# Macaron block on one core: the FFN's engine order listed from block 0's up product, nine more Strassen quads in each FFN, 31 of its first sums made by adding DMAs

## Chip, cores and metric

One NeuronCore of a Trainium2 chip. The metric is the device time of one execution in microseconds, taken as the median of three runs. Everything is fp32; a product is made from fp32r halves.

## What is computed

```python
f = _swiglu(_rmsnorm(h, ln_ffn1_pre), ffn1_gate, ffn1_up, ffn1_down)   # (silu(x@Wg) * (x@Wu)) @ Wd
h = h + 0.5 * _rmsnorm(f, ln_ffn1_post)
mx = _hybrid_mixer(_rmsnorm(h, ln_mix_pre), w_in, ...)                 # RWKV-7 scan and pooling
h = h + _rmsnorm(mx, ln_mix_post)
f = _swiglu(_rmsnorm(h, ln_ffn2_pre), ffn2_gate, ffn2_up, ffn2_down)
h = h + 0.5 * _rmsnorm(f, ln_ffn2_post)
```

There are 256 tokens of width 2048, and the FFN is 5632 wide. So each FFN reads three weights of 2048 x 5632 once.

## The kernel before

**A product in three matmuls.** Each fp32 operand is split into a high fp32r part H and a rest L. `mm3` (L317 to L321) makes one product of a 128-row slice as H·H, H·L and L·H, three matmuls with 512 columns. ScalarE casts H out of the loaded weight, and VectorE subtracts to get L (`fetch`, L373 and L383, two 128-row slices k at a time: 128 x 1024 elements). The tiles wH and wL come from a ring of five.

**Seven products for eight.** `seven` (L508) works on two blocks of 512 output columns at once, named f and l: gate and up in the first part of an FFN, two column blocks of the down weight in its second part. A letter f or l in its order string is a *pair*: two k of one weight for both halves of the tokens, 12 matmuls. A letter q is a *quad*: two k of both weights, by Strassen's scheme in 7 products (21 matmuls) where two pairs take 24. A quad costs VectorE more: it makes sums of weights, t13 (128 x 1024, L576), t2 and t4 (128 x 512 each, L581 and L585), and takes L from four tiles, a (1024), b (512), t13 and t24 (1024 each) (L598). The matching sums of the tokens (`sums`, L421) are made once for two quads and kept. After the last quad of a block the products' banks are merged on VectorE (L645, L693).

**Stages of an FFN.** Block 0 is the first 512 columns of gate, then of up; blocks 1 to 10 are gate and up together (`GATE_UP`, one order string for each); then the down product in two groups of 1024 output columns (`DOWN`). While block 0 is computed the normed tokens are scaled (`normed`), after each block the result is turned by VectorE, moved across partitions by 16 DMAs from GpSimd (L892) and split (`carry`). `post` makes the closing RMS norm, whose last column block is worked in two halves of tokens (`by_half`). The mixer between the FFNs uses `seven` once, with 4 quads (`OUT`).

**What sets the order.** `Plan` takes a list of operations with engine, cost, dependencies, buffers and due times, plays it through (`solve`) and emits each engine's instructions in that order. Before, the list begins with block 1; block 0, the statistics and the setup of the mixer are emitted outside it. All loads go out on SP's queue in the planned order. The constants at the top (`FETCH`, `UNITS`, `LAT`) are the planner's; 25 units of 4 KB a partition hold sums, kept tiles and loads.

Of the kernel before, what the change touches and what calls it, by code (L numbers as in the profile page):

```python
# [17 lines left out]
P = 128  # L18
# [26 lines left out]
DOWN = ((0, "fffffffffffqfff" "qllqllqllqllqllqllqll", 0),  # L45
        (2, "fqflqfqflqfqflqfqflqfqfqff", TRAIL))
OUT = ((0, "", 0), (1, "fffqfq" "qlqlll", 0), (3, "", TRAIL))
GATE_UP = ["", "ffffffffllllllll"] + ["ffqfqfqlqlll", "fffqffqlqllll", "ffqfqfqlqlll", "fffqffqlqllll", "ffqfqfqlqlll", "fffqffqlqllll", "ffqfqfqlqlll", "fffqffqlqllll", "ffqfqfqlqlll"]
SUMS = (2, 2)
BY_DMA = range(0)  # L50
LAT = dict(PE=0.22, DVE=0.1, ACT=0.17, SP=0.0, POOL=8.0)
AGAIN = dict(PE=0.0, DVE=0.0, ACT=0.0, SP=0.0, POOL=0.0)
UNITS = dict(ffn=25, out=22)
FIFO = dict(pt=4, pm=4, tmp=TB)
SPARE, KEEP, URGENT, HOLD = 3, 4, 8.0, 99
SOON, FETCH, LATEST, BEFORE = 22.0, 22.0, 12.0, 12.0
EARLY = 0.5
NXSPARE = 1
# [31 lines left out]
class Plan:  # L90


    def __init__(s):
        s.fifos = {r: [] for r in FIFO}
        s.nodes, s.last, s.chain, s.clk = [], None, {}, 0.0
        s.units, s.inserts = UNITS["out"], []
        s.begin = s.pe(BEFORE, lambda: None)
# [39 lines left out]
    def solve(s):  # L137
# [16 lines left out]
        free = dict(w32=[0.0] * W32_BUFS, ring=[BEFORE - 12 * MM * i for i in range(WS_BUFS)][::-1], unit=[0.0] * s.units)  # L154
# [29 lines left out]
        while len(order) < len(s.nodes):  # L184
            best = None
            for e, c in front.items():
                got = [(when(n), n) for n in c]
                if got:
                    first = min(a for a, _ in got)
                    a, n = min((x for x in got if x[0] <= first + 1e-9),  # L190
                               key=lambda x: x[1].due)
                    if best is None or a < best[0]:
                        best = (a, n)
# [27 lines left out]
class Block:  # L221
    def __init__(s, tc, ctx):
# [5 lines left out]
        s.late, s.after = [], []  # L228
# [38 lines left out]
    def run(s):  # L267

        E = mybir.EngineType
        with s.tc.manual_schedule(engines={E.PE, E.Activation, E.DVE, E.SP, E.Pool}):  # L270
            for n in s.plan.solve():
                n.fn()
            s.stats()
        s.plan, s.ready = Plan(), {}
# [42 lines left out]
    def mm3(s, ps, aH, aL, bH, bL, start, stop):  # L317
        nc = s.nc
        nc.tensor.matmul(ps, aH, bH, start=start, stop=False)  # L319
        nc.tensor.matmul(ps, aH, bL, start=False, stop=False)  # L320
        nc.tensor.matmul(ps, aL, bH, start=False, stop=stop)  # L321
# [80 lines left out]
    def by_half(s, w, c0, k0, k1, do, keep, done=None, deps=(), used=None, ready=None):  # L402
# [3 lines left out]
        for h in range(2):  # L406
            for k in range(k0, k1, 2):
                low, dst = got[k]
                at = []
                if ready is not None:  # L410
# [3 lines left out]
                         [low, *deps, *at],  # L414
# [6 lines left out]
    def sums(s, T, Td, j, out, own=None, nq=2, used=(), x32=None):  # L421
# [13 lines left out]
        def second():  # L435
            x = tt["x"] if x32 is None else x32[0][0].rearrange(
                "p (a b) t -> p a b t", b=2)[:, :nq]
            a11, a21 = x[:, :, 0, :P], x[:, :, 0, P:]
            a12, a22 = x[:, :, 1, :P], x[:, :, 1, P:]
            f = tt["f"] = s.unit((P, 4, nq, P), F32, "sf")  # L440
            V.scalar_tensor_tensor(out=f[:, 0], in0=a21, scalar=-1.0, in1=a22, op0=ALU.mult,
                                   op1=ALU.subtract)
            V.scalar_tensor_tensor(out=f[:, 1], in0=f[:, 0], scalar=-1.0, in1=a11,
                                   op0=ALU.mult, op1=ALU.subtract)
            V.tensor_tensor(out=f[:, 2], in0=a11, in1=a21, op=ALU.subtract)
            V.tensor_tensor(out=f[:, 3], in0=a12, in1=f[:, 1], op=ALU.subtract)
# [53 lines left out]
        else:  # L500
            b = p.op("DVE", 4 * cost("DVE", size / 4), second, [Td[j], p.chain.get("sums")],
                     [kf], [x32[1]], ahead=SOON, spare=NXSPARE)
        c = p.op("ACT", cost("ACT", size, 0.1 * (n - 1)), steps[0], [b, *used], kept)
# [4 lines left out]
    def seven(s, wf, cf, wl, cl, at, dep, KT, need, sm, order, ev_f, ev_l, used, trail=0):  # L508
# [4 lines left out]
        n = order.count("q")  # L513
# [4 lines left out]
        left = dict(f0=std + n, f1=std, l0=std + n, l1=std + n, p1=n, p5=n, p6=n, p7=n)  # L518
# [9 lines left out]
        def mul(b, x, wt):  # L528
# [5 lines left out]
            s.mm3(bank[b], *x, *wt, new, left[b] == 0)  # L534
# [9 lines left out]
        def pair(k, w, c0, b, by_dma):  # L544
            low, dst = s.fetch(w, k, c0, keep, by_dma, by_dma)

            def do():
                for i in range(2):
                    for h in range(2):
                        mul(f"{b}{h}", rows(k + i, h), ws[k + i])  # L550
            d = p.pe(12 * MM, do, [low, dep(k)] + claim(b + "0", b + "1"), dst)
# [3 lines left out]
        def quad(q):  # L555
# [10 lines left out]
            def get(m):  # L566
                i, x_ = m // 2, "ab"[m % 2]
                if m < 2:
                    v[x_] = raw((ka, kb)[m])
                w, c0 = ((wl, cl), (wf, cf))[(m + i) % 2]  # L570
                nc.sync.dma_start(out=v[x_][:, i],
                                  in_=w[(k + i) * P:(k + i + 1) * P, c0:c0 + 512])

            def t13():
                v["t13"] = s.unit((P, 2, 512), F32, "t13")
                V.tensor_tensor(out=v["t13"], in0=v["a"],  # L576
                                in1=v["b"][:, :1].to_broadcast([P, 2, 512]), op=ALU.subtract)
# [6 lines left out]
            def t4():  # L584
                V.tensor_tensor(out=v["t24"][:, 1], in0=v["b"][:, 1], in1=v["t24"][:, 0],  # L585
                                op=ALU.subtract)
# [9 lines left out]
            def low(n_, m):  # L596
# [3 lines left out]
            ld = [p.op("SP", 0.4, lambda m=m: get(m), take=([ka], [kb], (), ())[m], size=0.26,  # L600
                       chain="SP", ahead=FETCH) for m in range(4)]

            def half(n_, m, deps, rel):
# [5 lines left out]
            n13 = p.op("DVE", two, t13, ld[:3], [k13, k24], [ka, kb])  # L609
            la, ra = half("a", 2, [ld[0], ld[2]], [ka])  # L610
            n2 = p.op("DVE", one, t2, [n13], (), [ka, k13])
# [7 lines left out]
                                  mul("f0", S_(4), x["a"][1])),  # L619
                 [la, ds, dep(k)] + claim("p1", "f0", "f1"), ra)  # L620
            p.pe(3 * MM, lambda: mul("l0", rows(k + 1, 0), x["b"][0]),
                 [lb] + claim("l0", "l1"), rb)
# [3 lines left out]
            d = p.pe(6 * MM, lambda: (mul("p6", S_(2), x["t24"][0]),  # L626
                                      mul("l1", rows(k + 1, 1), x["t24"][1])),
                     [l24] + claim("p6"), r24)
# [13 lines left out]
        def add(o, b, i):  # L642
            if u[o] is None:
                new(o)
            V.tensor_tensor(out=u[o], in0=bank[b], in1=u[i], op=ALU.add)  # L645
        m, use = {}, {}

        def merge(d):
            for i in range(4):
                use[i] = p.claim("tmp")  # L650
            m["u0"] = p.op("ACT", cost("ACT", 512), copy, [d] + use[0][0])
            held["p1"].append(m["u0"])
            d = m["u0"]
            for o, b, i in ((1, "p6", 0), (2, "p7", 1), (1, "p5", 1), (3, "p5", 2)):
                d = m[f"u{o}"] = p.op("DVE", one, lambda o=o, b=b, i=i: add(o, b, i),
                                      [d] + (use[o][0] if o > 1 or b == "p6" else []))
                held[b].append(d)
                use[i][1].append(d)
        nq, last = 0, {}
        ks = dict(f=iter(range(K0, KT, 2)), l=iter(range(K0, KT - trail, 2)))  # L660
        for c in order:
            if c == "q":
                last["q"] = quad(nq)
                nq += 1
                if nq == n:
                    merge(last["q"])
# [7 lines left out]
            if c == "f" and left["f"] == std // 2:  # L674
                m["f"] = last["f"]

                def close_f():
                    for h, i in ((0, 1), (1, 3)):
                        if n:
                            d = p.op("DVE", one, lambda h=h, i=i: add(i, f"f{h}", i),  # L680
                                     [last["f"], m[f"u{i}"], last["q"]])
# [5 lines left out]
                if not n or "u3" in m:  # L687
# [4 lines left out]
        def total(h):  # L692
            V.tensor_tensor(out=u[2 * h], in0=bank[f"l{h}"], in1=u[2 * h], op=ALU.add)  # L693
        if trail:
            def finish(h, d):
                d = p.op("DVE", one, lambda: total(h), [d, m["u0"], m["u3"]], due=p.clk)
                ev_l(h, d, lambda: u[2 * h], None)
            s.by_half(wl, cl, KT - trail, KT, lambda k, h: mul(f"l{h}", rows(k, h), ws[k]),
                      keep, finish, [dep(k) for k in range(KT - trail, KT, 4)],
                      used)  # L700
            return
        for h in range(2):
            if n:
                d = p.op("DVE", one, lambda h=h: total(h), [p.last, m["u0"], m["u3"]])
                held[f"l{h}"].append(d)
                ev_l(h, d, lambda h=h: u[2 * h], use[2 * h][1])
# [3 lines left out]
    def head(s, w, c0, KT, do, keep, xs):  # L710
# [11 lines left out]
        with s.tc.manual_schedule(engines={E.PE, E.Activation, E.DVE, E.SP}):  # L722
# [27 lines left out]
            s.stats()  # L750

    def stats(s):
        while s.late:
            s.late.pop(0)()
# [70 lines left out]
    def rstd(s, ss, n, r):  # L825
        nc = s.nc
        t = s.small(1, "rt", bufs=2)
        nc.vector.tensor_reduce(out=t, in_=ss, axis=AX.X, op=ALU.add)
        t2 = s.small(1, "rt2", bufs=2)
        nc.vector.tensor_scalar(out=t2, in0=t, scalar1=1.0 / n, scalar2=NORM_EPS,  # L830
                                op0=ALU.mult, op1=ALU.add)
        nc.gpsimd.tensor_tensor(out=r, in0=t2, in1=s.mhalf[:, :1], op=ALU.pow)
# [48 lines left out]
    def carry_steps(s, T1, T, x32=None):  # L881

        nc = s.nc
        x, own = [x32], []
# [16 lines left out]
        def high(h):  # L901
            if h == 0:
                own.extend(s.new_T(1))
                T.extend(own)
# [27 lines left out]
    def carry(s, T1, T, turned, k1, by_dma=False):  # L932

        p = s.plan
        move, high, low, whole, minus, add = s.carry_steps(T1, T)
        kx, kT = Tok("unit"), [Tok("unit"), Tok("unit")]
        n = None
# [3 lines left out]
        hs = []  # L941
        for h in range(2):
            hs.append(p.op("ACT", cost("ACT", 512), lambda h=h: high(h), [n] + hs,
                           kT if h == 0 else (), chain="high",
                           spare=KEEP))
        if by_dma:
            for h in range(2):
                n = p.op("ACT", cost("ACT", 512), lambda h=h: whole(h), [n, *hs])
            n = p.op("ACT", cost("ACT", 1024), minus, [n, *hs])
            return p.op("POOL", 1.25, add, [n], (), [kx], size=0.94, lat=ADD), kT  # L950
# [38 lines left out]
    def ffn(s, wg, wu, wd, uT, rs, gpost, resid, emit, reload, xs=None):  # L989
        nc = s.nc  # L990
        hT, sm = [], [None] * 12
# [21 lines left out]
        s.gemm_tok(wg, 0, at, NKD, lambda h, ps: ev_g(0, h, ps), lead=True, xs=xs)  # L1013
# [1001 lines left out]
```

## Time and profile before

| what | value |
|---|---|
| three runs | 2016.54, 2017.03, 2017.33 us; median 2017.03 |
| span of the profiled execution | 2015.4 us, 1.6 us less than the median |
| TensorE instructions | 9957, busy 2000.9 us |
| VectorE / ScalarE / GpSimd busy | 1824.7 / 1192.3 / 327.6 us |
| FFN 1, mixer, FFN 2 (rough borders) | 31 to 707, 707 to 1326, 1326 to 2004 us |

Engines in the profile: PE is TensorE's matmul, PEld its weight load, DVE VectorE, ACT ScalarE, POOL GpSimd, SP the queue of loads. A row of the groups gives line, engine, operation, tiles (out<-in), shape, count, then busy time, mean ns of one, and the idle time before them. A row of the windows gives, for a stretch, the busy time of each engine, the granted clock, the DMA engines' busy share and GB/s. In the timeline the first figure is the start, the second the duration in us, and "xN" merges N instructions. Matmuls are pipelined, so the distance of two starts tells the pace, not the duration of one.

### The profile page before, as it was taken

How to read it: one execution, taken by the hardware profiler on the slowest of the kernel's cores; microseconds unless marked ns; L12 is line 12 of the kernel's file. 1: busy time of each engine (PE TensorE's matmuls, PEld its weight loads, DVE VectorE, ACT ScalarE, POOL GpSimd, SP SyncE). 2: the span in 40 equal slices, each digit the busy share in tenths (PEclk: the TensorE clock that was granted, in tenths of full speed). 3: DMA queues.
4: the chain of work that ended last, by engine and by line, in shares of the span. 5: the costliest groups of instructions: out<-in, count | busy, mean ns of one | idle time of the engine just before them, and what ended most of it. 6: DMA issues, size and time to landing. Idle time of an engine off the chain costs nothing.

```text
span 2015.4 us, 28684 instructions
## 1 busy us (share of the span) xinstructions
PE 2000.9 (99%) x9957; PEld 1655.1 (82%) x9957; DVE 1824.7 (91%) x2424; ACT 1192.3 (59%) x1586; POOL 327.6 (16%) x673
## 2 busy tenths in 40 slices
PE   9999999999999999999999999999999999999997
PEld 7888888888888888888788788888888888888886
DVE  6999999999999957789689678979999999999997
ACT  7555665556666566685476434665656555566663
POOL 0111211131000123403220111011113111310000
PEclk9999999999999999999999999999999999999999
DMA  7675674667568577757456547666656747665683
GB/s 268 224 241 182 220 242 160 218 213 241 175 203 299 209 212 214 205 175 214 146 173 190 159 168 269 244 216 215 228 198 218 245 142 235 211 228 183 207 294 126
DMA packets 227419, 423.56 MB, mean 210 GB/s; under 512 B 24639, under 2 KB 28105, under 8 KB 227273
## 3 DMA queue, kind: packets, MB, share of 16 engines
q1 hardware_dynamic: 204713, 384.70, 57.9%
q0 software_dynamic: 22272, 36.51, 5.5%
q8 instruction: 78, 1.28, 0.3%
q10 hardware_dynamic: 288, 0.52, 0.1%
q14 instruction: 68, 0.56, 0.1%
HBM read 396.69 MB, written 8.39 MB: 201 GB/s over the span
## 4 chain that ended last, share of the span: by engine, by line
PE 97%; DVE 1%; issue 1%; DMA 0%; ACT 0%; POOLq 0%; POOL 0%; DVEq 0%; ACTq 0%
PE mm L319 27%; PE mm L321 26%; PE mm L320 26%; PE ms L320 5%; PE ms L321 5%; PE ms L319 5%; PE tr L849 1%; PE pA L1733 0%; DVE u L645 0%; PE mc L817 0%; DMA x<-in_x_dram 0%; PE pU L1829 0%; PE pSa L1841 0%; PE pY L1864 0%; PE pT L1900 0%
## 5 line engine op out<-in xcount | busy, mean ns | idle before, releaser
L319 PE MATMUL mm<-wH,xH 128*128 128x512 f32 (+1 forms) x2116 | 825.5, 391 | 0.0
L320 PE MATMUL mm<-wL,xH 128*128 128x512 f32 (+1 forms) x2116 | 821.2, 388 | 0.0
L321 PE MATMUL mm<-wH,xL 128*128 128x512 f32 (+1 forms) x2116 | 821.1, 388 | 0.0
L319 PEld LDWEIGHTS mm<-wH,xH 128*128 128x128 f32 x2116 | 397.4, 188 | 82.1
L321 PEld LDWEIGHTS mm<-wH,xL 128*128 128x128 f32 x2116 | 397.4, 188 | 82.0 <-DVE xL L867 0.2
L373 ACT CAST wH<-w 128x1024 fp32r<-128x1024 f32 x313 | 326.2, 1054 | 231.7 <-PE mm L321 208.1
L320 PEld LDWEIGHTS mm<-wL,xH 128*128 128x128 f32 x2116 | 397.7, 188 | 79.7
L383 DVE TENSOR_TENSOR wL<-w,wH 128x1024 fp32r<-128x1024 f32 x313 | 373.0, 1218 | 18.9 <-ACT wH L373 17.3
L593 ACT CAST wH<-t 128x1024 fp32r<-128x1024 f32 x208 | 219.4, 1055 | 217.0 <-PE mm L321 108.9
L296 DVE TENSOR_TENSOR wL<-w,wH 128x1024 fp32r<-128x1024 f32 (+2 forms) x200 | 236.6, 1192 | 95.7 <-ACT wH L295 94.1
L295 ACT CAST wH<-w 128x1024 fp32r<-128x1024 f32 (+2 forms) x200 | 205.4, 1034 | 170.9 <-PE mm L321 150.7
L892 POOL DMA_DIRECT2D x<-T x352 | 173.1, 499 | 729.8 <-DVE T L875 190.3
L598 DVE TENSOR_TENSOR wL<-t,wH 128x1024 fp32r<-128x1024 f32 x208 | 248.6, 1217 | 0.7 <-ACT wH L593 0.7
L593 ACT CAST wH<-w 128x1024 fp32r<-128x1024 f32 x208 | 168.3, 835 | 56.6 <-PE mm L321 30.0
L598 DVE TENSOR_TENSOR wL<-w,wH 128x1024 fp32r<-128x1024 f32 x208 | 194.5, 951 | 0.3
L576 DVE TENSOR_TENSOR t<-w,w 128x1024 f32<-128x1024 f32 x104 | 126.7, 1218 | 0.0
L320 PE MATMUL ms<-wL,sH 128*128 128x512 f32 x276 | 107.6, 390 | 0.2
L319 PE MATMUL ms<-wH,sH 128*128 128x512 f32 x276 | 107.4, 389 | 0.0
L321 PE MATMUL ms<-wH,sL 128*128 128x512 f32 x276 | 107.4, 389 | 0.0
L585 DVE TENSOR_TENSOR t<-w,t 128x512 f32<-128x512 f32 x104 | 71.8, 690 | 2.6
L581 DVE TENSOR_TENSOR t<-w,t 128x512 f32<-128x512 f32 x104 | 71.3, 686 | 0.6
L645 DVE TENSOR_TENSOR u<-ms,u 128x512 f32<-128x512 f32 x92 | 61.4, 686 | 1.4
(317 smaller groups left out, 2107.8 us busy)
## 6 DMA issues: line engine op xcount, KB each, us to landing
w<-in_w_in_dram SPq DMA_DIRECT2D x128, 512.0 KB
w<-in_ffn_up_dram SPq DMA_DIRECT2D x112, 512.0 KB
w<-in_ffn_gate_dram SPq DMA_DIRECT2D x110, 512.0 KB
w<-in_ffn_down_dram SPq DMA_DIRECT2D x104, 512.0 KB
w<-in_ffn_down_dram SPq DMA_DIRECT2D x144, 256.0 KB
w<-in_ffn_gate_dram SPq DMA_DIRECT2D x132, 256.0 KB
w<-in_ffn_up_dram SPq DMA_DIRECT2D x128, 256.0 KB
w<-in_w_out_dram SPq DMA_DIRECT2D x24, 512.0 KB
```

Source lines behind the costliest of these rows:

```text
L295: s.nc.scalar.copy(vH, v)
L296: s.nc.vector.tensor_tensor(out=vL, in0=v, in1=vH.bitcast(F32), op=ALU.subtract)
L319: nc.tensor.matmul(ps, aH, bH, start=start, stop=False)
L320: nc.tensor.matmul(ps, aH, bL, start=False, stop=False)
L321: nc.tensor.matmul(ps, aL, bH, start=False, stop=stop)
L373: nc.scalar.copy(x["H"], x["v"])
L383: nc.vector.tensor_tensor(out=x["L"], in0=x["v"], in1=x["H"].bitcast(F32), op=ALU.subtract)
L576: V.tensor_tensor(out=v["t13"], in0=v["a"], in1=v["b"][:, :1].to_broadcast([P, 2, 512]), op=ALU.subtract)
L585: V.tensor_tensor(out=v["t24"][:, 1], in0=v["b"][:, 1], in1=v["t24"][:, 0], op=ALU.subtract)
L593: nc.scalar.copy(H, src)
L598: V.tensor_tensor(out=L, in0=src, in1=H.bitcast(F32), op=ALU.subtract)
L892: nc.gpsimd.dma_start(out=x[0][q * 32:q * 32 + 32, i], in_=src[i * 32:i * 32 + 32, q])
```

## The change

1. **More quads.** The order strings change, from 50 quads in each FFN to 59 (41 in blocks 1 to 10, two of them in block 1, and 18 in the down product). Block 1 works on the normed tokens as the others do.
2. **Adding DMAs.** A capital Q is a quad whose t13 VectorE does not add: SP loads the two slices into t13, and a DMA from GpSimd then adds the third slice, 512 KB broadcast over both halves, to it in SBUF. The slices a and b are loaded besides, so such a quad loads 5 slices of 256 KB on SP's queue and not 4. There are 31 in each FFN, 24 of them in blocks 1 to 10. Signs are turned so that the sum is an addition.
3. **The list starts earlier.** Block 0's up product, the sums of squares and their powers, the spread of the norm, `normed` and the mixer's setup (whose 12 small loads go from SP's queue to GpSimd's) are operations of the plan.
4. **Merges.** In the last down group the quads' banks are added into the PSUM bank before the last pairs run on, so no sum is left after the last matmul; in one block of each FFN bank l1 is seeded with a sum. The FFN's last squares are summed on ScalarE and no longer on VectorE. The token sums of five of the down product's groups start from a kept fp32 copy, and one addition falls away.
5. **Planner.** VectorE work that uses the result just before it is charged 0.12 us (`AGAIN`), an operation that is due sooner may be awaited 0.13 us (`PATIENCE`).

```diff
-GATE_UP = ["", "ffffffffllllllll"] + ["ffqfqfqlqlll", "fffqffqlqllll", ...]
+GATE_UP = ["", "fffflQlfqfllll", "fqqflQQQfll", "flflQfqqQfll", "flqQfffqQlll", ...]
+            def begin():
+                v["t13"] = s.unit((P, 2, 512), F32, "t13")
+                for i, (w, c0) in enumerate(((wf, cf), (wl, cl))):
+                    nc.sync.dma_start(out=v["t13"][:, i],
+                                      in_=w[(k + i) * P:(k + i + 1) * P, c0:c0 + 512])
+            def adding():
+                nc.gpsimd.dma_start(out=v["t13"], in_=wl[k * P:(k + 1) * P, cl:cl + 512]
+                                    .unsqueeze(1).to_broadcast([P, 2, 512]), accum_op=ALU.add)
...
+            if far:
+                n13 = p.op("SP", 0.8, begin, take=[k13], size=0.52, ahead=FETCH)
+                n13 = p.op("POOL", 1.0, adding, [n13], size=0.94, lat=FAR)
-            n2 = p.op("DVE", one, t2, [n13], (), [ka, k13])
+            n2 = p.op("DVE", one, t2, [n13, ld[0]], [k24] * far, [ka, k13])
...
-        part, direct = [None, None], KT == NKD
+        part, direct = [None, None], True
```

**VectorE in a gate and up block of FFN 1.** Before, in a stretch of two quads: every t13 is made by L576 from two loaded tiles w.

```order
L576 TENSOR_TENSOR t_689_3062<-w_659_2892,w_666_2925 128x1024
L581 TENSOR_TENSOR t_692_3067<-w_659_2892,t_689_3062 128x512
L598 TENSOR_TENSOR wL_3065<-t_685_3026,wH_3064 128x1024
L585 TENSOR_TENSOR t_692_3067<-w_666_2925,t_692_3067 128x512
L576 TENSOR_TENSOR t_696_3081<-w_676_2980,w_677_2982 128x1024
L383 TENSOR_TENSOR wL_3079<-w_652_2868,wH_3078 128x1024
L383 TENSOR_TENSOR wL_3088<-w_655_2873,wH_3087 128x1024
L598 TENSOR_TENSOR wL_3100<-w_659_2892,wH_3099 128x1024
```

In the changed program, at the quads t_571 and t_639 of FFN 1 (L622, L627, L631, L644 are the lines that were L576, L581, L585, L598):

```order
L644 TENSOR_TENSOR wL_2749<-w_596_2560,wH_2748 128x512
L627 TENSOR_TENSOR t_637_2753<-w_599_2567,t_571_2437 128x512
L622 TENSOR_TENSOR t_639_2757<-w_609_2611,w_611_2618 128x1024
L631 TENSOR_TENSOR t_637_2753<-w_604_2588,t_637_2753 128x512
L627 TENSOR_TENSOR t_642_2775<-w_609_2611,t_639_2757 128x512
L644 TENSOR_TENSOR wL_2772<-t_557_2396,wH_2771 128x1024
L631 TENSOR_TENSOR t_642_2775<-w_611_2618,t_642_2775 128x512
```

The quad of t_571 has no L622: its L627 takes a t13 that a DMA has summed. Quads stand closer, and the plain pairs' L383 between them are fewer.

**GpSimd in the same part.** Before, only the moves of `carry` stand there, 16 for a block:

```order
L892 DMA x_384_1654<-T_379_1629 32x256 x16
L892 DMA x_477_2069<-T_471_2036 32x256 x16
L892 DMA x_553_2423<-T_550_2405 32x256 x16
L892 DMA x_658_2887<-T_647_2836 32x256 x16
L892 DMA x_722_3180<-T_717_3160 32x256 x16
```

Now (L982 is the move, L617 the adding DMA):

```order
L982 DMA x_519_2206<-T_506_2153 32x256 x16
L617 DMA t_557_2396<-in_ffn_up_dram 128x2x512
L617 DMA t_571_2437<-in_ffn_up_dram 128x2x512
L982 DMA x_603_2583<-T_583_2498 32x256 x16
L617 DMA t_600_2569<-in_ffn_up_dram 128x2x512
L617 DMA t_626_2705<-in_ffn_up_dram 128x2x512
L617 DMA t_643_2777<-in_ffn_up_dram 128x2x512
```

Adding DMAs and moves share GpSimd's queue, each behind the one before.

**VectorE at the program's end.** Before, for the last half of the tokens: the total (L693), the squares (L1173), the gain (L1159), the outputs (L1182).

```order
L693 TENSOR_TENSOR u_18796<-mm_18047,u_18796 128x512
L1173 ISA junk_18939,rt_2610_13152<-u_18796,rp_18871 128x512
L1173 ISA rt_2610_13152 128x1
L1159 TENSOR_TENSOR fg_13146<-u_18796,gb_13142 128x512
L1182 SCALAR_TENSOR_TENSOR fg_13145<-fg_13145,rs_13151,h_163_694 128x512 x2
L1182 SCALAR_TENSOR_TENSOR fg_13146<-fg_13146,rs_13151,h_164_695 128x512 x2
```

Now, from the first half's outputs on (L1291 the gain, L1302 the norm, L1314 the outputs; ScalarE's squares of mm_18553 stand between L1291 and L1302):

```order
L1314 SCALAR_TENSOR_TENSOR fg_13103<-fg_13103,rs_13109,h_113_447 128x512 x2
L1314 SCALAR_TENSOR_TENSOR fg_13104<-fg_13104,rs_13109,h_114_448 128x512 x2
L1291 TENSOR_TENSOR fg_13106<-mm_18553,gb_13102 128x512
L1302 TENSOR_SCALAR rt_2618_13112<-ss_13108,rp_19186 128x1
L1314 SCALAR_TENSOR_TENSOR fg_13105<-fg_13105,rs_13111,h_115_449 128x512 x2
L1314 SCALAR_TENSOR_TENSOR fg_13106<-fg_13106,rs_13111,h_116_450 128x512 x2
```

The total after the last matmul has gone, and the gain reads the PSUM bank ahead of the squares.

More of the change, by code (lines that the diff above doesn't have):

```diff
@@ L652, in merge, with step @@
             held["p1"].append(m["u0"])
[L653 to L656, printed above, removed]
+            def step(o, b, i, after):
+                d = m[f"u{o}"] = p.op("DVE", one, lambda: add(o, b, i), after + (
+                    use[o][0] if o > 1 or b == "p6" else []))
@@ L941, in carry @@
         hs = []
+        keep.append((x, kx, n))
         for h in range(2):
             hs.append(p.op("ACT", cost("ACT", 512), lambda h=h: high(h), [n] + hs,
[L944 to L950, printed above, removed]
+                           kT if h == 0 else (), chain=None if late else "high",
+                           spare=KEEP, ahead=SOON if late else 1e9))
         for h in range(2):
@@ L1110, in normed @@
         done, toks, own = [], [], {}
-        rows = p.op("ACT", 2.0, lambda: None, [p.begin])
         for i in range(len(uT)):
```

483 lines of the change are left out of this document (306 added, 177 removed).

## Prediction

> **What bounds the kernel now.** I read the page's shares first, then the windows by stage, then the waits of PE. In the page, PE and DVE are the two engines to think of:
>
> ```profile
> span 2015.4 us, 28684 instructions
> PE 2000.9 (99%) x9957; PEld 1655.1 (82%) x9957; DVE 1824.7 (91%) x2424; ACT 1192.3 (59%) x1586; POOL 327.6 (16%) x673
> ```
>
> A PE that is 99% busy need not run at its peak, so its pace comes from the timeline. The first and the last of 77 matmuls in a row, in FFN 1:
>
> ```profile
> 599.72 0.39 PE L320 MATMUL ms<-wL,xH 128*128 128x512 f32 x1
> ...
> 616.95 0.39 PE L321 MATMUL ms<-wH,sL 128*128 128x512 f32 x1
> ```
>
> 76 steps in 17.23 us are 0.2267 us each, for quads and pairs alike. The waits of PE, in full, show that nothing holds this pace up for long:
>
> ```profile
> PE warm L725 <- POOL ident masks.py:199: 1.7, 1, 1.7
> PE tr L849 <- DMA x<-in_x_dram: 1.2, 1, 1.2
> PE pU L1829 <- DVE R L1854: 0.3, 1, 0.3
> ```
>
> The first two are the start of the program, the third is in the mixer. So in the FFNs the time is the number of matmuls times 0.2267 us. How far DVE is from becoming the bound, the windows show: the two FFNs, then their steady parts in the gate and up blocks, and the first 50 us of FFN 2. The columns are the length, then the busy time of PE, PEld, DVE, ACT and POOL, the clock, the DMA engines' share and GB/s.
>
> ```profile
> 31.00:707.00 676.00, 675.89 (x2999) 559.56 (x2998) 658.55 (x778) 405.25 (x487) 97.33 (x194) 1.00 0.65 219
> 1326.00:2004.00 678.00, 677.89 (x2994) 561.14 (x2993) 649.99 (x762) 401.58 (x479) 93.94 (x185) 1.00 0.63 212
> ...
> 100.00:500.00 400.00, 400.00 (x1766) 331.21 (x1765) 395.26 (x455) 237.46 (x269) 78.58 (x160) 1.00 0.65 216
> 1330.00:1380.00 50.00, 50.00 (x223) 41.37 (x222) 36.05 (x40) 29.55 (x43) 11.21 (x18) 1.00 0.79 268
> 1430.00:1830.00 400.00, 400.00 (x1766) 331.35 (x1765) 395.67 (x461) 238.21 (x272) 70.67 (x144) 1.00 0.63 207
> ```
>
> PE is never idle in the steady parts, and DVE only for 4.7 and 4.3 us of 400. In the whole FFNs DVE is idle for 17.5 and 28.0 us, 14 of the latter in FFN 2's first 50 us.
>
> **The quads.** Nine more in each FFN are 18, and each needs 21 matmuls where two pairs need 24. That is 54 matmuls less, in the order too, and 54 x 0.2267 = 12.24 us off PE. All of it lies on the path as long as PE keeps its pace.
>
> **What DVE does instead.** The counts are differences of the two programs' orders, the durations these groups:
>
> ```profile
> L383 DVE TENSOR_TENSOR wL<-w,wH 128x1024 fp32r<-128x1024 f32 x313 | 373.0, 1218 | 18.9 <-ACT wH L373 17.3
> L598 DVE TENSOR_TENSOR wL<-t,wH 128x1024 fp32r<-128x1024 f32 x208 | 248.6, 1217 | 0.7 <-ACT wH L593 0.7
> L576 DVE TENSOR_TENSOR t<-w,w 128x1024 f32<-128x1024 f32 x104 | 126.7, 1218 | 0.0
> L585 DVE TENSOR_TENSOR t<-w,t 128x512 f32<-128x512 f32 x104 | 71.8, 690 | 2.6
> L598 DVE TENSOR_TENSOR wL<-w,wH 128x512 fp32r<-128x512 f32 x104 | 71.2, 684 | 0.0
> L645 DVE TENSOR_TENSOR u<-ms,u 128x512 f32<-128x512 f32 x92 | 61.4, 686 | 1.4
> L433 DVE TENSOR_TENSOR sx<-xH,xL 128x1024 f32<-128x1024 f32 x12 | 14.6, 1219 | 0.0
> ```
>
> Removed: 44 sums t13 (104 become 60; 62 of the 122 quads are summed by DMA) at 1.218 us, 53.6 us; 18 rests of plain loads at 1.218, 21.9; 10 joins sx at 1.219, 12.2; four closing squares and four gated products in block 1, about 6 at the price of a 128x512 operation and a little more. Together 93.7 us. Added: 36 sums t2 and t4 at 0.69, 24.8 us; 36 rests of t at 1.217, 43.8; 18 rests of 128x512 at 0.684, 12.3; 18 operations of merging, gating and seeding at 0.686, 12.3; and about 2.8 for one more group of token sums. Together 96.0 us. The balance is +2.3 us for both FFNs, 1.2 each: the adding DMAs pay nearly all that the quads cost DVE.
>
> So each FFN gets 6.1 us shorter on PE and 1.2 us longer on DVE, and DVE has to give up 7.3 us of idle time to follow. If all its idle time can be filled (17.5 and 28.0 us), PE never waits. If only that of the steady parts can (4.7 and 4.3), PE waits for 2.6 + 3.0 = 5.6 us. I take **2.6 us**, nearer the first, by two rows: the list now begins with block 0's up product and block 1 has two quads, which is work for the 14 us in which DVE idles at 1330 to 1380; and DVE's busy time overlaps itself a little, since two operations of 1.22 us take 2.35 us end to end:
>
> ```profile
> 1985.84 2.35 DVE L383 TENSOR_TENSOR kL<-w,kH 128x1024 fp32r<-128x1024 f32 x2
> ```
>
> One more such operation costs 1.13 us, so there is room under "busy" that the window doesn't show.
>
> **ACT and SP.** ACT casts 36 more tiles t and 18 small ones and 18 fewer plain ones, at the 1.05 and 0.62 us of its rows below about 30 us on 1192; at 59% busy that stays hidden, though DVE waits for ACT where a cast comes late.
>
> ```profile
> L593 ACT CAST wH<-w 128x1024 fp32r<-128x1024 f32 x104 | 109.4, 1052 | 37.1 <-PE mm L321 25.8 <-DMA w<-in_ffn_down_dram 4.7 <-DVE u L645 2.3
> L593 ACT CAST wH<-w 128x512 fp32r<-128x512 f32 x104 | 64.3, 618 | 19.6 <-issue 5.4 <-PE mm L321 4.2 <-ACT u L1067 3.8
> ```
>
> The mixer's 12 small loads leave SP's queue for POOL's; the plan puts them ahead of the first adding DMA, and PE has no gap there that they could fill or open. The mixer's own matmuls are the same.
>
> **The adding DMAs.** None stands in the trace of before, so their price is bounded. The queues, and the landings of POOL's transfers of the same 512 KB:
>
> ```profile
> q1 hardware_dynamic: 204713, 384.70, 57.9%
> q0 software_dynamic: 22272, 36.51, 5.5%
> ...
> gb<-in_ln_ffn_post_dram POOLq DMA_DIRECT2D x4, 512.0 KB, 6.8
> xr<-in_x_dram POOLq DMA_DIRECT2D x4, 512.0 KB, 8.9
> ```
>
> 384.7 MB in 57.9% of 2015.4 us is 330 GB/s at a full share. In a steady part 24 quads load 0.26 MB more each (6.3 MB, 19 us of all engines) and add 0.52 MB (12.6 MB, 38 us, or 76 if an added byte costs two). On 400 us the share of 0.65 becomes 0.79, at most 0.89: not a bound, but less room. Landing: 6.8 to 8.9 us as plain transfers, 13.6 to 17.8 at twice that; I take about 11, in the gap between, since only the adding reads its target too. How much time there is follows from SP's order: between the loads of a quad's base and those of its tile a stand at least 2.36 MB (8 of the 62 quads), up to 2.88 MB for 25. With a's own 0.52 MB and 216 GB/s that is 13.3 and 15.7 us. So I price the adding at nothing; t2 would wait behind a late one, with all of DVE's queue after it, and on POOL the moves of `carry` stand behind it, whose results are used only in the down product.
>
> **The end.** After the last matmul, before: total, squares, root; in the new order: gain, then squares on ACT. The first row below is the total, the third the first output; the mixer's end shows the new order.
>
> ```profile
> 2004.54 0.69 DVE L693 TENSOR_TENSOR u<-mm,u 128x512 f32<-128x512 f32 x1 [5.59 <-PE mm L321]
> ...
> 2007.08 2.74 DVE L1182 SCALAR_TENSOR_TENSOR fg<-fg,rs,h 128x512 f32<-128x512 f32 x4 [0.44 <-POOL rs L1178]
> ```
>
> ```profile
> 1305.27 0.69 DVE L1159 TENSOR_TENSOR fg<-mm,gb 128x512 f32<-128x512 f32 x1 [1.14 <-PE mm L321]
> ...
> 1307.68 2.74 DVE L1182 SCALAR_TENSOR_TENSOR fg<-fg,rs,h 128x512 f32<-128x512 f32 x4 [0.69 <-POOL rs L1178]
> ```
>
> From the last matmul's sum to the first output it took 2.54 us, and 2.41 in the new order: -0.1 us, which I leave out. The total that is saved comes back because ACT's squares wait for the gain on the same bank.
>
> **The sum.** The profiled span of 2015.4 us lies 1.6 us under the median of 2017.03, which is outside the span and stays. 2015.4 - 12.24 + 2.6 = 2005.8 us of span, 2007.4 us of time, 0.48% less.
>
> **Rivals.**
>
> *DVE sets the pace already.* PE and DVE are both full in the steady parts, and it may be that PE only looks free because the plan has fitted the two together. Then none of the 7.3 us per FFN can be had, PE waits for 14.6 us, and the time is 2017.0 - 12.2 + 14.6 = 2019.4 us, no change. For it: 395 of 400 us busy. Against it: PE steps at 0.2267 us throughout and has no wait for DVE in an FFN that is worth a row. The Trainium skill (Perfetto Trace Analysis, Identifying the Most-Contended Engine) says that PE's busy share is a poor measure and that its weight loads' share, 82% here, is better, while DVE's occupancy is a fair one; by that, DVE is the most contended of the two in the FFNs, and this rival is the likely case. The trace has a pace that doesn't change with what DVE does, so I give it 0.13.
>
> *The adding DMAs land late.* DVE's queue is in order: where t2 waits for its t13, all rests behind it wait, and PE after five ring tiles. With DVE full, a wait isn't won back. At a landing of x us the 8 shortest leads lose x - 13.3 each and the 17 next x - 15.7. From 14.5 us on that eats the gain of 9.6 us; at 15.7 us it is 8 x 2.4 = 19 us, and the time 2026.6 us, slower. For it: twice the plain landing is 13.6 to 17.8 us, and the DMA share rises. Against it: the plain landings are half of the lead. The skill (DMA: Bandwidth & Descriptors, Rules for kernel authors) says that an accumulating DMA reads its target and writes it later, which speaks for the dearer end; no trace here shows it yet. I give it 0.10.
>
> *Small new waits.* PE waits inside `seven` for a seed or a merged bank, a chain of three DVE operations of 0.69 us behind the last quad, in 23 blocks, some 0.3 us each, on top of the 5.6 us: 2017.0 - 12.2 + 12.5 = 2017.3 us at worst, 2014 in the middle. 0.07.
>
> **Chances.** The forecast, with PE's waits between 0 and 8 us, has 0.70 and runs from 2004.5 to 2012.8 us. What a measurement of this kernel can tell from no change is about 0.2%, 4 us: 2013.0 to 2021.1 us. Below it lie the forecast's 0.70, and 0.04 of the small waits and of a half-way first rival; above it most of the late adding, 0.10; the rest, 0.16, is the same. The range reaches from 2004.0 us (all 12.2 us, and the end's 0.1 with some spread) to 2017 us, which takes in the small waits and leaves out some 0.2.
>
> **What the profile after would show.** PE with 54 matmuls less, the same 0.2267 us step, and waits for DVE of 1 to 4 us in each FFN, at the rests or sums of quads; DVE at 98% of an FFN, with the idle time of 1330 to 1380 filled; L617 landing in 8 to 14 us; the mixer as long as before. If L627 waits for DMA, or L617 lands after more than 14 us, the second rival holds. If PE waits for DVE by 7 us in each FFN while DVE has no gap, the first does.

## The result, and the profile after

| | before | after |
|---|---|---|
| median of five runs | 2017.03 us | 2006.44 us (2005.37 to 2009.14) |
| ratio, 95% interval | | 0.9949 [0.9937, 0.9961] |
| profiled execution: time, span | span 2015.4 us | 2005.37 us, span 2003.7 us |

The kernel became faster by 10.6 us in the median and 11.7 us in the two profiled spans; the profiled execution after is the fastest of its five. The page of after, its span and the engines' shares:

```profile
span 2003.7 us, 29050 instructions
PE 1990.0 (99%) x9903; PEld 1644.7 (82%) x9903; DVE 1813.6 (91%) x2462; ACT 1224.3 (61%) x1631; POOL 410.0 (20%) x747
```

PE has 54 instructions less (9957 - 9903). Its pace, from the first and the last of 77 matmuls in a row in FFN 1:

```profile
589.74 0.39 PE L333 MATMUL ms<-wL,xH 128*128 128x512 f32 x1
...
606.97 0.39 PE L334 MATMUL ms<-wH,sL 128*128 128x512 f32 x1
```

17.23 us for 76 steps are 0.2267 us again. The waits of PE (us in total, times, longest us):

```profile
PE mm L332 <- ACT wH L386: 1.5, 1, 1.5
PE warm L809 <- POOL ident masks.py:199: 1.4, 1, 1.4
PE tr L939 <- DMA x<-in_x_dram: 0.6, 2, 0.4
PE mm L332 <- DVE u L703: 0.5, 1, 0.5
PE pU L1977 <- DVE R L2002: 0.3, 1, 0.3
PE ms L333 <- DVE wL L644: 0.2, 1, 0.2
```

One row is new and over 1 us, the first. The timeline shows where it lies:

```profile
25.68 3.49 DVE L1249 TENSOR_TENSOR nx<-xH,xL 128x1024 f32<-128x1024 f32 x3
...
27.84 0.40 PE L332 MATMUL mm<-wH,xH 128*128 128x512 f32 x1
28.60 2.96 ACT L386 CAST wH<-w 128x1024 fp32r<-128x1024 f32 x3
29.08 1.22 DVE L309 TENSOR_TENSOR wL<-w,wH 128x1024 fp32r<-128x1024 f32 x1
29.73 0.50 PE L332 MATMUL mm<-wH,xH 128*128 128x512 f32 x1 [1.49 <-ACT wH L386]
```

At the start of FFN 1, DVE makes three of `normed`'s joins (L1249) ahead of a rest wL (L309) of the weight. PE's matmuls stand 1.89 us apart there, and a second gap of 0.63 us follows. The profile names ACT's cast as the releaser: since the rest comes late, PE's order takes the H·H of the next weight ahead and meets that one's cast.

The windows: the FFNs, then the stretches that were shown of before:

```profile
31.00:701.00 670.00, 670.00 (x2968) 554.69 (x2967) 651.93 (x798) 420.42 (x506) 139.25 (x250) 1.00 0.83 255
1320.00:1992.00 672.00, 671.84 (x2973) 556.06 (x2972) 646.48 (x784) 417.94 (x502) 130.78 (x218) 1.00 0.81 251
100.00:500.00 400.00, 400.00 (x1767) 331.20 (x1766) 398.59 (x481) 253.59 (x286) 107.54 (x183) 1.00 0.86 260
1326.00:1376.00 50.00, 50.00 (x223) 41.37 (x222) 43.69 (x55) 33.36 (x46) 2.36 (x3) 1.00 0.83 278
1430.00:1830.00 400.00, 400.00 (x1767) 331.31 (x1766) 396.20 (x476) 253.37 (x292) 107.60 (x183) 1.00 0.84 256
```

PE is never idle in the steady parts. DVE has 1.4 and 3.8 us of idle time left there, and 18.1 and 25.5 us in the whole FFNs. The DMA share rose from 0.65 to 0.86 in FFN 1's steady part.

The queues, the adding DMAs among the DMA issues (the last figure is the median us to landing), and the landings of all L617 together:

```profile
q1 hardware_dynamic: 213984, 400.89, 60.4%
q0 software_dynamic: 39520, 69.08, 15.3%
...
t<-in_ffn_up_dram POOLq DMA_DIRECT2D x48, 512.0 KB, 8.4
...
DMA to landing us min/median/max: 5.9/7.4/12.5
```

They land like plain transfers of that size (6.8 and 8.9 us before). The tightest, from its issue to the t2 that uses it (the trace pairs 54 of the 62):

```profile
1795.06 1.28 POOL L617 DMA_DIRECT2D t<-in_ffn_down_dram  x1
1812.55 0.69 DVE L627 TENSOR_TENSOR t<-w,t 128x512 f32<-128x512 f32 x1
```

That is 17.5 us of time for a transfer of 12.5 us at most; the median of these leads is 29.0 us.

The end of the program: the first sum after the last matmul, the outputs and their DMAs, of after and then the DMAs of before:

```profile
1994.88 0.69 DVE L1291 TENSOR_TENSOR fg<-mm,gb 128x512 f32<-128x512 f32 x1 [5.33 <-PE mm L334]
...
1997.26 2.74 DVE L1314 SCALAR_TENSOR_TENSOR fg<-fg,rs,h 128x512 f32<-128x512 f32 x4 [0.66 <-POOL rs L1310]
1998.04 2.32 SPq L2126 DMA_DIRECT2D out_dram<-fg  x4
```

```profile
2007.86 2.32 SPq L1978 DMA_DIRECT2D out_dram<-fg  x4
```

From the first output's DMA to the end of the span it takes 2003.7 - 1998.0 = 5.7 us now and took 2015.4 - 2007.9 = 7.5 us before. This is 1.9 us of the gain in the spans, and these four DMAs are the same in both. What the end waits for stands in the closing drains of GpSimd's and SP's queues (duration in ns, minimum, median and maximum, then the first and the last start in us; the longest drain of GpSimd is its first), of before and then of after:

```profile
L2010 POOLq DRAIN  x3: 46/98/8569, 2006.1 to 2015.2; - x3
L2010 SPq DRAIN  x3: 7/7/47, 2013.3 to 2014.9; - x3
```

```profile
L2158 POOLq DRAIN  x3: 46/97/4351, 1996.6 to 2003.4; - x3
L2158 SPq DRAIN  x3: 7/7/7, 2002.8 to 2003.1; - x3
```

Before, GpSimd's drain lasts 8.57 us, to 2014.6, and SP, which has waited for the outputs, is at its own drain 1.3 us earlier. Now GpSimd's drain lasts 4.35 us and is over at 2001.0, and SP comes last.

### The profile page after: what moved, and what is told of

It reads as the page before. It is cut to its first block, busy times and chain, and to the rows that moved or that the text cites. A ratio compares the mean times of both kernels' runs of the same rounds, so it can differ in the third digit from the quotient of the medians.

```text
span 2003.7 us, 29050 instructions
## 1 busy us (share of the span) xinstructions
PE 1990.0 (99%) x9903; PEld 1644.7 (82%) x9903; DVE 1813.6 (91%) x2462; ACT 1224.3 (61%) x1631; POOL 410.0 (20%) x747
## 3 DMA queue, kind: packets, MB, share of 16 engines
q0 software_dynamic: 39520, 69.08, 15.3%
## 4 chain that ended last, share of the span: by engine, by line
PE 93%; DVE 3%; DMA 2%; issue 1%; ACT 0%; SPq 0%; DVEq 0%; POOLq 0%; POOL 0%; ACTq 0%
PE mm L332 25%; PE mm L334 24%; PE mm L333 24%; PE ms L333 5%; PE ms L334 5%; PE ms L332 5%; DMA w<-in_ffn_down_dram 1%; DVE wL L644 1%; PE tr L939 1%; DVE wL L396 1%; DMA w<-in_w_out_dram 0%; PE pA L1881 0%; DVE t L622 0%; PE mc L901 0%; DVE t L627 0%
## 5 line engine op out<-in xcount | busy, mean ns | idle before, releaser
L332 PE MATMUL mm<-wH,xH 128*128 128x512 f32 (+1 forms) x2008 | 784.3, 391 | 2.0 <-ACT wH L386 1.5
L334 PE MATMUL mm<-wH,xL 128*128 128x512 f32 (+1 forms) x2008 | 779.4, 388 | 0.1
L333 PE MATMUL mm<-wL,xH 128*128 128x512 f32 (+1 forms) x2008 | 779.3, 388 | 0.1
L334 PEld LDWEIGHTS mm<-wH,xL 128*128 128x128 f32 x2008 | 377.0, 188 | 78.7 <-DVE xL L957 1.1
L333 PEld LDWEIGHTS mm<-wL,xH 128*128 128x128 f32 x2008 | 377.3, 188 | 75.7 <-DVE wL L309 0.4
L639 ACT CAST wH<-t 128x1024 fp32r<-128x1024 f32 x244 | 257.1, 1055 | 221.2 <-PE mm L334 121.0
L396 DVE TENSOR_TENSOR wL<-w,wH 128x1024 fp32r<-128x1024 f32 x293 | 351.9, 1227 | 13.8 <-ACT wH L386 12.5
L644 DVE TENSOR_TENSOR wL<-t,wH 128x1024 fp32r<-128x1024 f32 x244 | 295.7, 1234 | 10.9 <-ACT wH L639 10.2
L309 DVE TENSOR_TENSOR wL<-w,wH 128x1024 fp32r<-128x1024 f32 (+2 forms) x184 | 217.5, 1190 | 84.6 <-ACT wH L308 83.2
L982 POOL DMA_DIRECT2D x<-T x352 | 180.6, 608 | 389.6 <-DVE T L965 76.1
L644 DVE TENSOR_TENSOR wL<-w,wH 128x1024 fp32r<-128x1024 f32 x244 | 231.6, 966 | 0.9 <-ACT wH L639 0.9
L617 POOL DMA_DIRECT2D t<-in_ffn_up_dram x48 | 59.8, 1256 | 230.8 <-DMA t<-in_ffn_up_dram 56.1
L631 DVE TENSOR_TENSOR t<-w,t 128x512 f32<-128x512 f32 x122 | 85.5, 701 | 0.5 <-DMA w<-in_ffn_down_dram 0.2
L627 DVE TENSOR_TENSOR t<-w,t 128x512 f32<-128x512 f32 x122 | 85.3, 700 | 0.3 <-DMA w<-in_ffn_down_dram 0.3
L622 DVE TENSOR_TENSOR t<-w,w 128x1024 f32<-128x1024 f32 x60 | 73.8, 1231 | 2.8 <-DMA w<-in_ffn_down_dram 2.8
```

Source lines behind the costliest of these rows:

```text
L309: s.nc.vector.tensor_tensor(out=vL, in0=v, in1=vH.bitcast(F32), op=ALU.subtract)
L332: nc.tensor.matmul(ps, aH, bH, start=start, stop=False, skip_group_check=seeded)
L333: nc.tensor.matmul(ps, aH, bL, start=False, stop=False, skip_group_check=seeded)
L334: nc.tensor.matmul(ps, aL, bH, start=False, stop=stop, skip_group_check=seeded)
L396: nc.vector.tensor_tensor(out=x["L"], in0=x["v"], in1=x["H"].bitcast(F32), op=ALU.subtract)
L627: V.tensor_tensor(out=v["t24"][:, 0], in0=v["a"][:, 0], in1=v["t13"][:, 1], op=ALU.add)
```

## Experiments

**The changed kernel again.** No edit.

> The changed kernel itself once more, unaltered, as the mark for the others and to see its spread: its five timed runs lay 3.8 us apart (2005.37 to 2009.14 us), those of the kernel before 1.1 us. Theory: the spread belongs to the kernel, because DVE has 1.4 us of idle time left in 400 us of an FFN and any lateness of a sum reaches PE; then the runs lie over 2 us apart again, with a median of 2005.4 to 2007.5 us. Rival: it was that chip or that hour; then they lie within about 1 us.

Measured: 2005.83 us (2004.62 to 2008.37). The spread of 3.8 us is there again, so it was not that chip or that hour. It isn't this program's alone either: the kernel before had 2.7 us over the 14 runs beside these (2016.68 to 2019.41), and the kernel with 52 plain quads below has 4.3 us without an adding DMA. Nor is the theory's reason at work where it can be looked up: of the unaltered changed kernel, an execution of 2009.03 us was profiled too, beside the second run with 7 us below. The first 100 us of the execution of 2005.37 us, and of that one:

```profile
0.00:100.00 100.00, 96.22 (x428) 78.31 (x429) 84.34 (x123) 63.58 (x103) 25.41 (x68) 1.00 0.86 284
```

```profile
0.00:100.00 100.00, 94.85 (x412) 76.61 (x413) 80.97 (x119) 62.61 (x102) 22.84 (x67) 0.97 0.83 276
```

PE is 16 matmuls behind after 100 us, which at 0.2267 us each are 3.6 us, all that separates the two spans (2003.7 and 2007.3 us); in the steady part from 100 to 500 us both have 1767 matmuls and DVE the same idle time. The granted clock is 0.87 from 10 to 20 us in the slower one, and 1.00 in the other. In its 15 timed runs the changed kernel has a mean clock of 0.999 whenever the time is at most 2006.44 us, and 0.997 or 0.998 whenever it is longer. What lowers the clock at the start is not shown.

**The joins later, by 9 us.**

```diff
+        s.edge = EDGE if xs else 0.0
         nT, nTd, nTk, nx = s.normed(uT, rb, rows, uTk)
...
-            n = p.op("DVE", cost("DVE", 1024), join, (), [kx])
+            n = p.op("DVE", cost("DVE", 1024), join, (), [kx], early=s.edge)
```

> The three joins of the residual (1024 elements each, 3.49 us in all) that the changed kernel's DVE does at the start of FFN 1, ahead of the first second halves of the up product, get a due time there again and go behind these; FFN 2 keeps its order. Theory: the waits of 1.89 and 0.63 us of PE at 27.8 and 29.7 us, the only new wait of the trace of after, are these joins; the kernel takes 2.0 to 2.5 us less, about 2004.1 us against 2006.4. Rival: PE waits there for the casts of ACT, as the releaser in the trace has it, or the joins only move the wait to the quads behind them: no more than 0.5 us less, or some us more.

Measured: 2007.22 us (2006.55 to 2009.47). The time is 1.4 us over that of the unaltered kernel in the same group (2005.83): by the number the rival's "some us more", but not by its reason. The wait for the cast is gone, and the new ones are not at the quads behind the joins, but in the mixer:

```profile
PE pA L1882 <- DVE R L1858: 1.3, 2, 1.1
PE pB L1901 <- DVE R L1893: 1.1, 2, 0.8
PE mm L332 <- ACT sgb L1518: 0.6, 1, 0.6
```

The same stretch of the mixer in the changed kernel and here (three waits, 2.9 us of PE):

```profile
860.00:900.00 40.00, 40.00 (x240) 33.22 (x238) 37.56 (x58) 31.35 (x60) 1.57 (x3) 1.00 0.53 166
```

```profile
863.00:903.00 40.00, 37.09 (x220) 30.06 (x218) 37.69 (x57) 29.84 (x55) 1.57 (x3) 1.00 0.46 146
```

PE's order in the mixer is the same, that of ACT and DVE is not. This part stands outside the lists, and a simulated timeline sets its order, so an edit in FFN 1 reached it. What decides between the two orders there was not found. The profiled execution is also one with a low clock at the start (0.91 in the first 20 us).

**The joins later, by 7 us.** The same edit with `s.edge = 7.0 if xs else 0.0`; a due time at which the mixer's order stays that of the changed kernel.

> The joins of FFN 1 late once more, with a due time of 7 us in place of 9: on DVE they go behind the same first rests of the up product, ACT's whole order and the mixer's orders on PE, ACT and DVE stay those of the changed kernel (with 9 us ACT and DVE changed places with each other in 39 rows of the mixer). Theory: the joins cost PE 2.3 us, and what the second run lost (2.5 us in the mixer's first half and 1.3 us near the end of FFN 2) came with the mixer's other order: no wait at 27 to 30 us, the mixer as in after, about 2003.5 us (2002.5 to 2005). Rival: DVE has the 3.5 us of joins to do anyway and gives them back to PE later in FFN 1 or at its end; no gain, 2005.5 to 2007.5 us.

Measured: 2003.39 us (2002.73 to 2006.09). The waits of PE hold neither the cast nor the mixer's three (the rows left out have 0.3 us and less):

```profile
PE warm L809 <- POOL ident masks.py:199: 1.4, 1, 1.4
PE mm L334 <- DVE xL L957: 0.7, 2, 0.5
PE mm L332 <- DVE u L703: 0.5, 1, 0.5
PE tr L939 <- DMA x<-in_x_dram: 0.4, 1, 0.4
...
```

The two kernels were then run on one chip beside each other.

> The changed kernel unaltered, beside the next run on one chip, so that the two can be set against each other: so far their medians come from different groups of runs. Expected by both theories: 2005.4 to 2006.5 us.

> The joins by 7 us once more, beside the changed kernel. Theory, that the joins cost PE 2.3 us at the start of FFN 1 and are not paid again elsewhere: 1.8 to 2.8 us under the run before it, about 2003.4 us. Rival, that the gain of the first such run was scatter (the runs of one kernel lie up to 3.8 us apart): within 1 us of it.

Measured: 2005.99 us (2005.40 to 2009.03) for the changed kernel, 2003.72 us (2002.32 to 2004.65) with the late joins, 2.3 us less. In its first 100 us PE has 438 matmuls in the first of the two runs with 7 us, 10 more than the changed kernel's 428, and 10 matmuls are 2.3 us. So the joins are the one wait over 1 us that the change added, and this version beats both kernels: 0.9933 [0.9920, 0.9945] of the time before.

**52 plain quads.** The order strings are those of the kernel before from block 2 on, with two quads in block 1 and no adding DMA:

```diff
-GATE_UP = ["", "fffflQlfqfllll", "fqqflQQQfll", "flflQfqqQfll", ...]
+GATE_UP = ["", "fffflqlfqfllll"] + ["ffqfqfqlqlll", "fffqffqlqllll", ...]
-SUMS = (2, 2, 1)
+SUMS = (2, 2)
```

> The changed code with the order of the kernel before in the FFNs' later blocks: 50 quads in each FFN there and two in block 1, all first sums on DVE and no adding DMA. Theory, that the gain is the matmuls that quads save at 0.2267 us each: 14 quads fewer than after are 42 matmuls more, 9.5 us, about 2016 us (2014.5 to 2017). Rival, that the gain comes from the other edits (statistics in the order, DVE lighter by the first sums' absence, norms elsewhere): no matmul's price shows and the time stays within 2 us of 2006.4 us. Second rival, that half of the gain is elsewhere: about 2011 us.

Measured: 2022.32 us (2021.99 to 2026.3), dearer than any theory said. Its page and the outputs' DMAs:

```profile
span 2020.6 us, 28612 instructions
PE 1999.8 (99%) x9945; PEld 1651.5 (82%) x9945; DVE 1825.1 (90%) x2446; ACT 1200.0 (59%) x1601; POOL 331.9 (16%) x685
```

```profile
2012.07 2.32 SPq L2123 DMA_DIRECT2D out_dram<-fg  x4
```

Of the 16.9 us more in the span, 42 matmuls are 9.5. The mixer has the other order, with the same three waits as in the run with 9 us, 1.3, 1.1 and 0.6 us: 3.0. The end after the first output's DMA is 2.9 (8.5 against 5.7 us), with a drain of 9.17 us on GpSimd's queue in place of 4.35; 1.3 of the 1.5 us left are smaller waits of PE. The matmuls' price is there as the theory has it, and two things came on top that no matmul explains. The other edits bring nothing without the quads: this kernel has four quads more than the kernel before (12 matmuls, 2.7 us) and is 5.1 us slower (2017.24 us in the runs beside it); of these 7.8 us the mixer's order and the end are 4.0, the joins 2.3.

**The first sums back on DVE.** The order in the FFNs stays; the body of the adding operation becomes an addition on DVE (the tile to itself).

```diff
-                nc.gpsimd.dma_start(out=v["t13"], in_=wl[...].to_broadcast([P, 2, 512]), accum_op=ALU.add)
+                V.tensor_tensor(out=v["t13"], in0=v["t13"], in1=v["t13"], op=ALU.add)
```

> The changed kernel in its own order, with the adding DMA of each of its 62 marked quads (31 in each FFN) replaced by a DVE addition of the same 1024 elements at the same place of the program (it adds the tile to itself, so the sums are not the reference's). Theory: DVE, with 1.4 us of idle time in 400 us after the change, has no room: 31 x 1.135 = 35.2 us more in each FFN against 18.1 and 25.5 us of idle time in all, so PE waits for DVE for at least 17.1 + 9.7 = 27 us in all, and up to 70 us if the idle time lies where nothing can be moved into it: 2033 to 2076 us. Rival: DVE had room that the union of its rows hides (its operations overlap by 182 us in all), so that the adding DMAs buy nothing: 2006 to 2010 us.

Measured: 2068.74 us (2065.87 to 2069.81). The first theory holds, at its upper end: 62.9 us over the 2005.83 us of the changed kernel in the same group of runs for 62 x 1.135 = 70.4 us of additions. Not all of it is the additions' price. The mixer has the other order here too, with the same three waits of 3.0 us, and the end is 8.6 us long in place of 5.7, with GpSimd's drain at 9.17 us. That leaves at most 57 us, 0.92 us for each sum. DVE's idle time took little of it: over the whole span it fell by 5 us, from 190 to 185. The steady part, and the waits of PE:

```profile
100.00:500.00 400.00, 385.03 (x1648) 305.30 (x1647) 399.70 (x470) 235.05 (x268) 70.64 (x144) 1.00 0.64 213
```

```profile
PE ms L333 <- DVE wL L644: 11.0, 22, 1.3
PE mm L332 <- DVE u L703: 8.2, 8, 1.9
PE mm L332 <- DVE u L778: 7.6, 11, 2.1
```

**Copying in place of adding.** `accum_op=ALU.add` is left out of the DMA.

> The adding DMA of each marked quad copies the same 512 KB into t13 without adding (so t13 is the third slice alone, not the sum). Nothing else moves. Theory: an added byte costs the DMA engines twice a copied one (6.0 against 3.04 us of one engine's share per MB), but they bound nothing: the share of 100 to 500 us falls from 0.86 to about 0.77, that of GpSimd's queue from 15.3% to about 10.4%, and the time stays within 1.5 us of the changed kernel's. Rival: the traffic of the adding itself slows DVE and delays loads, and the 1% by which DVE's operations have become longer is its price; then DVE's mean of a 1024-element operation goes back from 1.228 to 1.218 us and the time falls by 2 us or more, to 2004 or less.

Measured: 2007.17 us (2004.46 to 2008.14), within the 1.5 us of the theory. The changed kernel was not run in this group; in three others its median was 2005.83 to 2006.44 us. Queue, steady part, landing:

```profile
q0 software_dynamic: 31584, 69.08, 10.8%
...
100.00:500.00 400.00, 400.00 (x1767) 331.21 (x1766) 398.55 (x481) 253.78 (x286) 95.57 (x183) 1.00 0.77 257
...
DMA to landing us min/median/max: 3.9/5.4/9.3
```

The theory's 0.77 and 10.4% came out as 0.77 and 10.8%: adding costs the DMA engines nearly twice as much a byte, and 2 us of landing, and the kernel shows no price for either. The adding DMAs go in twice as many packets (272 each against 144), but that isn't what makes them dear: SP's loads, whose packets are as small (1.9 KB on average), take 3.0 us of all the engines' time for each MB, the copying DMAs 3.2 and the adding ones 6.0, worked out from the queues' shares. The rival falls: DVE's durations went to 1.213 us here, but they differ as much between executions of the changed kernel, which had 1.218 us in its next one.

**Adding twice.** The adding DMA is issued a second time behind the first.

> Each of the 62 adding DMAs is issued twice in a row (the third slice is added twice, so t13 is not the reference's sum), and the planner doesn't know it. Theory, by the doubled price of an added byte: in a steady part 24 quads add 12.6 MB more at 6.0 us of one engine's share per MB, 76 us of 400, so the DMA share of 0.86 would be 1.05: loads and sums come late, PE waits at least 5% of some 1300 us in the FFNs, and the time is 2050 us or more, with L617 landing after 14 us and L627 waiting for it. Rival, an added byte costs as a copied one and the lead of 13.3 us holds: share 0.95, landing below 13 us, time within 4 us of the changed kernel's.

Measured: 2082.3 us (2080.8 to 2085.11). The steady part, and t2 (L629 here, x122; busy and mean ns, then DVE's idle time ahead of it):

```profile
100.00:500.00 400.00, 375.39 (x1610) 306.32 (x1609) 363.94 (x431) 228.24 (x254) 123.82 (x181) 0.97 0.97 268
```

```profile
L629 DVE TENSOR_TENSOR t<-w,t 128x512 f32<-128x512 f32 x122 | 83.1, 682 | 63.1 <-DMA t<-in_ffn_up_dram 54.8 <-issue 6.1 <-DMA t<-in_ffn_down_dram 1.3
```

The second adds (L619): GpSimd's idle time ahead of them with the number of times, and their landings; and PE's longest wait:

```profile
  DMA t<-in_ffn_up_dram: 283.3, 37
...
DMA to landing us min/median/max: 5.7/9.1/11.4
```

```profile
PE ms L333 <- DVE wL L646: 32.0, 11, 10.6
```

The size is the theory's, the way only partly. The adds landed after 8.8 (L617) and 9.1 us in the median, not after 14; but the second writes the same tile and waits on GpSimd's queue until the first has landed, so together they take some 18 us, as long as the tightest lead, and the queue falls behind. The DMA share is 0.97 besides. The mixer's other order is here too, 2.9 us of the some 76 by which this kernel is longer. Which of the two weighs more is left open; what is shown is that the t2 that waits for its DMA costs PE tens of us, and that one add fits where two don't.

## Why the prediction came out right

The forecast was 2007.4 us, the median is 2006.4.

- **Pace and quads (-12.24 us): right.** 54 matmuls less at the same 0.2267 us.
- **PE's waits (+2.6 us): right in size, wrong in place.** From before to after, the first output moves from 2007.08 to 1997.26 us, by 9.8 us where the two terms make 9.6. But the waits were to lie in each FFN at rests or sums of quads, 1 to 4 us each. There, there is almost nothing (0.5 and 0.2 us in the rows). Of the 2.4 us that are missing from 12.24, 2.0 lie in the first 100 us, where PE has 428 matmuls and had 437. This is one place, the joins ahead of block 0's rests, and the run with late joins has 438 there. That the size fits is luck. The prediction listed `normed` among the operations that move into the plan and didn't price where its joins would go.
- **DVE's balance (+2.3 us, 7.3 us of idle time to give up in each FFN): the wrong measure.** Priced in durations it holds: their sum over all rows rose by 3.8 us (1971.6 to 1975.4) in the repeat of the changed kernel, whose mean of a 1024-element rest was 1.218 us as before. But the time in which DVE is occupied fell by 11.1 us (1824.7 to 1813.6), because operations that follow each other directly overlap, by 146.9 us in all before (1971.6 - 1824.7) and by 161.6 us in the repeat (1975.4 - 1813.8). The idle time of the FFNs hardly shrank (17.5 and 28.0 to 18.1 and 25.5 us). The 14 us at the start of FFN 2 became 6.3. So DVE followed PE by closing up, which the prediction had only as a remark on room under "busy".
- **Adding DMAs at nothing: right, and the cover is wide.** The DMA share came out nearer the dear bound (0.86 of 0.79 to 0.89), and the copying run shows the doubled price. Landing was 7.4 us where 11 was taken; the tightest lead 17.5 us where SP's order gave 13.3, since that counted only traffic between loads. Taking the sums back to DVE costs at most 57 us without the mixer's other order and the end: each add is worth some 0.9 us, most of a DVE step of 1.135.
- **The end (-0.1 us): the edit right, the rest unforeseen.** From the last matmul's sum to the first output, 2.54 us became 2.38. Another 1.9 us went after it, which no term had: the end no longer waits for GpSimd's drain. The drain takes 4.35 us in every run with 62 DMAs into t13 on GpSimd's queue, adding or copying, 5.66 with 124, and 9.17 when an edit of those operations alone takes them off it; why is not shown. The profiled span fell 2 us below the forecast of 2005.8 nearly by this alone. The median lies 2.7 us above that span, which is of the fastest of the five executions, and not 1.6 us as the sum took it. That these two unforeseen things, -1.9 and +1.1 us, pull against each other and leave the median within 1.0 us of the forecast is luck too.
- **The rivals.** *DVE sets the pace already* falls: a place for the Trainium skill's rule (Perfetto Trace Analysis, Identifying the Most-Contended Engine), by which DVE was the more contended; PE kept its step while DVE's busy time followed. It was near, though: with 35 us more in each FFN, DVE does set the pace. *The adding DMAs land late* falls here, and the run with two adds shows the mechanism as described. The Trainium skill (DMA: Bandwidth & Descriptors, Rules for kernel authors) says that an accumulating DMA reads its target and writes it later; it gives no price there, and the nearly doubled engine time fits it. *Small new waits* in the merges and seeds don't appear.

## What to carry to other kernels

When VectorE is full, work that a DMA can do (here a sum of weights) is worth most of its step on VectorE (0.9 of 1.135 us here), provided that the plan gives it time: compare the landing with the tightest lead from issue to use, and watch what stands behind it on GpSimd's queue. Judge an engine's room by the steps between operations, not by durations or the busy share. An edit to one part of a program whose order a scheduler makes can turn over another: set the orders of all engines, and the time behind the last output, side by side before a difference in time is put down to the edit.

## What the runs showed of the hardware

- An accumulating DMA into SBUF took nearly twice the DMA engine time of a copying one, 6.0 against 3.2 us of all engines for each MB. With 32.5 MB of adding, GpSimd's queue has a share of 15.3%, with the same bytes copied 10.8%, with none 5.5%. The landing of 512 KB had a median of 7.4 against 5.4 us, and its issue took GpSimd 1.26 us (the 48 of the up weight, mean) against 0.74.
- The time from the first output's DMA to the end of the program differs between programs though the outputs are the same: 5.7 us in after, 7.5 before, 8.5 with 52 quads, 8.6 with the sums on DVE. In the last three the end waits for GpSimd's drain, which took 8.57, 9.17 and 9.17 us; in after it took 4.35 and was over before the outputs' queue. Why it is shorter with the DMAs into t13 is not shown.
- With two adds, where PE stood still for up to 10.6 us at a time, its granted clock was 0.97 in the steady part. With the sums on DVE, where the waits were 2.1 us at most, it was 1.00 in the steady part.
- At the start, PE's longest wait for the tokens x was 0.4 to 1.3 us in seven of the eleven traces, and the granted clock from 10 to 20 us was 1.00 in all of these. In the other four the wait was 1.5 to 2.1 us and the clock 0.87 to 0.94. That the one brings the other is not shown.
